# Two-layer hybrid backbone on one core: raw slots of their own for the second half of the output weights, gate rows written to DRAM in the first branch, six first tiles in the last layer

## The chip, the cores and the metric

The kernel runs on one core of a Trainium2 chip. The metric is the device time of one launch in microseconds (us). Before the change the median of 3 runs is 2333.93 us (2331.47 to 2334.76).

## The reference, cut to what matters

Two layers work on 1024 latent tokens and 256 context tokens of width 1024, all in float32. Each layer normalizes and modulates its input, projects it into an attention, a convolution and a recurrent branch, and merges the three branches. The change touches only the merge and what follows it:

```python
y = stack([yb * silu(gb) for yb, gb in zip(ys, gs)])
proj = einsum('btnw,nwd->btnd', y, w_branch)          # three products 512 -> 1024
g = sigmoid(h @ w_gate + b_gate)                      # three gates per channel
out = sum(proj * g, over the branches) @ w_out        # the output product, 1024 -> 1024
x = layer_norm(ALPHA * x + gate * out) * ln_g + ln_b  # gate: one row per stream
```

The first layer does this for context and latent tokens, the last layer for latent tokens alone, since only they are returned. `gate` is a row of 1024 numbers; latent and context tokens have one each.

## The kernel before, in words

Every float32 product is made of three matmuls: each operand is split into a high part and a remainder (`hi`, `lo`), and hi*hi, hi*lo and lo*hi are added up in PSUM. A weight tile (class `Wt`, `load` at L330) costs one 512 KB DMA on SP's queue into a slot called `raw`, one ACT copy that makes `whi`, and one DVE subtraction that makes `wlo`. The pool `W` has NWL = 2 slots for `raw` and NW = 4 each for `whi` and `wlo`.

A layer has two phases. Phase 1 does the projections and the branches and leaves the branch outputs (`y_d`) and the gates (`th_d`) in DRAM. Phase 2 (L1140) does the merge in two stages:

- Branch stage (`gemm`, loop over `i, b in enumerate(BR)`): for each of three branches four weight units (`dp`), each with two output chunks (`dd`), each with the token groups: NT_C (256 context tokens, first layer only), NT_0 and NT_1 (512 latent tokens each). A group is 12 matmuls. DVE multiplies the PSUM result with the gate tile `thl`, which SP loads into three slots in turn, and adds it to `m`. In the third branch (`i == 2`) ACT and DVE split the finished chunk of `m` into the tiles that are the left operand of the output product.
- Output stage: the tokens are cut into tiles of 128 (ten in the first layer, eight in the last). A half (`half_of(q, ch)`) is the product of tile q with one half of the output columns, 24 matmuls in four steps `kp` of 6, each with one weight tile. `w0` (four tiles) is the first half of `w_out` and `w1` (four tiles) the second. Then DVE multiplies by the gate tile `gt`, adds the residual `xp` and takes statistics; after the second half `norm` normalizes the tile and writes it out.

The program text makes the weight tiles of the output stage in this order: `w0[0]` and `w0[1]`, fetched ahead in the branch stage; then, after the pool `a` of the branch stage is closed and the pool `c` opened in its place, `w1[0..3]`; then `w0[2]` and `w0[3]`. `w1` keeps `whi` and `wlo` in pool `c`, but its `raw` slots are the two of `W`. The halves are worked through in an order set by `first = 4`: the first halves of four tiles, their second halves, then both halves of each later tile.

Pool `a` holds, by address, three `yst` slots (6 KB per partition), three `thl` slots (6 KB) and the branch operands `yy`. Pool `c` reuses that room; a tile in it waits only for the tiles that it covers.

The gate row comes from `gate_rows` (L1130), called in the third branch: a PE transpose of a column tile, a DVE copy into `grow`, a DMA of `grow` to `gate_d` in DRAM, and two DMAs that read it back, spread over all partitions, into `gt`. In the first layer it is called after `dp` 1 (context) and `dp` 3 (latent), in the last after `dp` 0.

The order on each engine is fixed before the run. A planner (class `Driver`) picks by estimated times which stream emits its next step; a scheduler then goes by program order among the instructions whose operands and slots are ready in its own simulated time. A load can so be put ahead of earlier program text if its slot is free. On the chip each engine and each DMA-issuing queue then runs its list in order.

Of the kernel before, what the change touches and what calls it, by code (L numbers as in the profile page):

```python
# [8 lines left out]
F32 = mybir.dt.float32  # L9
# [26 lines left out]
NS, NHF, NW, NWL, NMX, NYST = 10, 14, 4, 2, 8, 3  # L36
# [153 lines left out]
def kernel(  # L190
# [12 lines left out]
    W = ctx.enter_context(tc.tile_pool(name="wts", bufs=1))  # L203
# [15 lines left out]
    def f32(ap):  # L219
        return ap.bitcast(F32)  # L220

    def psum(n=512, name="ps"):
        return PM.tile([128, n], F32, tag="mm", name=name, bufs=4)
# [97 lines left out]
    class Wt:  # L321
# [6 lines left out]
            self.ap, self.ready = drv_.side(lambda: self.load(src, a, b, home or W))  # L328

        def load(self, src, a, b, home):  # L330
            raw = W.tile([128, a, b], F32, tag="raw", name="raw", bufs=NWL)
            sp.dma_start(out=raw, in_=src)
            hi = home.tile([128, a, b], F32R, tag="whi", name="whi", bufs=NW)
            lo = home.tile([128, a, b], F32R, tag="wlo", name="wlo", bufs=NW)
            act.activation(out=hi, in_=raw, func=AF.Copy)
            dve.tensor_tensor(out=lo, in0=raw, in1=f32(hi), op=ALU.subtract)
            return hi, lo
# [789 lines left out]
        drv_.run([lru(), att_values(), att_scores(), lru_in(), lru_out(), att_proj(), att_out(), conv(), gates()], PRIO[l])  # L1127
        assert wlive[0] == 0 and sl.used == 0 and hl_.used == 0 and pl_.used == 0

    def gate_rows(l, s, dst):  # L1130

        row = SM.tile([128, 128], F32, tag="grow", name="grow")
        ps = psum()
        pe.transpose(ps[0:KD, 0:128], ada[l][:, 16:24, s], ident)
        dve.tensor_copy(row[0:KD], ps[0:KD, 0:128])
        sp.dma_start(out=gate_d[l][s].rearrange("(k p) -> k p", p=128), in_=row[0:KD])
        for i in range(2):
            sp.dma_start(out=dst[i], in_=gate_d[l][s][i * 512:i * 512 + 512].partition_broadcast(128))

    def phase2(l, open_a, open_b, open_c):  # L1140

        last = l == DEPTH - 1
        groups = [NT_0, NT_1] if last else [NT_C, NT_0, NT_1]
# [73 lines left out]
        gts, lnw = {}, []  # L1217

        def gemm():
            tfetch()  # L1220
            wfetch(2)
            ms, mg = {}, {}
            for i, b in enumerate(BR):
                for dp in range(4):
                    if i == 0:
                        for nt in groups:
                            if nt is NT_C:
                                ms[dp, 0] = mc("m").rearrange("p (d n) -> p d n", d=2)
                                continue
                            yield ("pe", xq.room())  # L1230
                            xq.take()
                            ms[dp, nt[0]] = mx("m", [128, 2, 512])
                    w = wnext()
                    wfetch(2)
                    for dd in range(2):
                        dch = dp * 2 + dd
                        for nt in groups:
                            ti, t0, n = nt
                            while (i, ti) not in yt_ or any(e[:2] == (i, nt) for e in yq):
                                yield ("act", drv_.t["pe"] + LAG_Y)  # L1240
                                ysplit()
                            if i == 2 and (ti not in mg):
                                mg[ti] = alloc_h(ti, n)
                            tfetch()
                            th = tq.pop(0)
                            yield ("pe", w.ready)
                            y = yt_[i, ti]
                            ps = psum()
                            c_ = 0
                            for k in range(4):  # L1250
                                for a, v in ((0, 0), (0, 1), (1, 0)):
                                    pe.matmul(out=ps[:, 0:n], lhsT=w[a][:, k, dd * 128:dd * 128 + 128], rhs=y[:, v, k, :],
                                              start=(c_ == 0), stop=(c_ == 11))
                                    c_ += 1
                                if k == 1:
                                    yield "pe"
                            mm = ms[dp, ti][:, dd, 0:n]
                            dst = mm if i == 0 else th[:, 0:n]
                            dve.scalar_tensor_tensor(out=dst, in0=th[:, 0:n], scalar=1.0, in1=ps[:, 0:n], op0=ALU.add,
                                                     op1=ALU.mult)  # L1260
                            if i:
                                dve.tensor_tensor(out=mm, in0=mm, in1=dst, op=ALU.add)
                            if i == 2:
                                split(mm, mg[ti][0][:, dch, :], mg[ti][1][:, dch, :])
                        if dp:
                            for _ in range((len(groups) + 1) // 2 if dd else len(groups) - (len(groups) + 1) // 2 + 1):
                                if yq and yq[0][0] == i + 1:
                                    yield "act"
                                    ysplit()
                    w.free()  # L1270
                    if i == 2:
                        xq.give(2)
                        if dp in ((0,) if last else (1, 3)):
                            s_ = 1 if dp == 1 else 0
                            gts[s_] = mc("gt"), mc("gt")
                            gate_rows(l, s_, gts[s_])
                        if dp == 3:
                            xq.take(2)
                            lnw.extend((mx("lng", [128, D]), mx("lnb", [128, D])))
                            sp.dma_start(out=lnw[0], in_=ln_g[l].partition_broadcast(128))  # L1280
                            sp.dma_start(out=lnw[1], in_=ln_b[l].partition_broadcast(128))
                        elif dp:
                            for _ in range(2):
                                xq.take()
                                xfetch()
            sa.close()
            sc, RC = open_c()
            pools.append((sc, RC))
            w1 = [Wt(w_out[l][kp * 256:kp * 256 + 256, 512:1024].rearrange("(k p) n -> p k n", p=128), 2, 512, RC)
                  for kp in range(4)]  # L1290
            w0 = [wnext() for _ in range(4)]
            sts = {}
            first = 4

            def half_of(q, ch):
                nt, t = tiles[q]
                ti, n = nt[0], nt[2]
                if ch == 0:
                    while len(xps) <= q:
                        yield ("pe", xq.room())  # L1300
                        xq.take()
                        xfetch()
                cq = slice(ch * 512, ch * 512 + 512)
                ws = (w0, w1)[ch]
                ps = None
                for kp in range(4):
                    yield ("pe", ws[kp].ready)
                    if ps is None:
                        ps = psum()
                    for k in range(2):  # L1310
                        for a, v in ((0, 0), (0, 1), (1, 0)):
                            pe.matmul(out=ps, lhsT=mg[ti][a][:, 2 * kp + k, t * 128:t * 128 + 128], rhs=ws[kp][v][:, k, :],
                                      start=(kp == 0 and k == 0 and a == 0 and v == 0), stop=(kp == 3 and k == 1 and a == 1))
                tt = RC.tile([128, 512], F32, tag="tt", name="tt", bufs=2)
                dve.tensor_tensor(out=tt, in0=ps, in1=gts[1 if ti == 0 else 0][ch], op=ALU.mult)
                dve.scalar_tensor_tensor(out=xps[q][:, cq], in0=xps[q][:, cq], scalar=ALPHA, in1=tt, op0=ALU.mult, op1=ALU.add)
                if ch == 0:
                    sts[q] = SM.tile([128, 2, 6], F32, tag="st1", name="st1", bufs=8)
                    ln_half(xps[q], sts[q], 0)
                else:  # L1320
                    fin.append((nt, t, xps[q], sts[q]))
                    if t == n // 128 - 1:
                        done.add(ti)

            order = [(q, ch) for ch in range(2) for q in range(first)]
            order += [(q, ch) for q in range(first, len(tiles)) for ch in range(2)]
            for q, ch in order:
                yield from half_of(q, ch)
            for w in w0 + w1:
                w.free()  # L1330
# [129 lines left out]
```

## Time and profile before

| | |
|---|---|
| median of 3 runs | 2333.93 us |
| profiled execution | 2332.71 us, span 2330.9 us, mean granted TensorE clock 0.986 |
| PE | 2257.4 us busy, 97% of the span, 11344 matmuls |
| DVE | 1679.5 us, 72% |
| ACT | 1003.3 us, 43% |
| POOL | 87.0 us, 4% |
| SP's DMA queue (q1) | 226.06 MB; ACT's (q10) 51.92 MB |

Phase 2 of the first layer runs from about 1022 to 1317 us, that of the last layer from about 2080 us to the end. PE is busy nearly throughout, so a change can gain only where PE stands still or runs at the lower of its two clock levels, or in the last 9 us, where it has finished.

### The profile page before, as it was taken

How to read it: one execution, taken by the hardware profiler on the slowest of the kernel's cores; microseconds unless marked ns; L12 is line 12 of the kernel's file. 1: busy time of each engine (PE TensorE's matmuls, PEld its weight loads, DVE VectorE, ACT ScalarE, POOL GpSimd, SP SyncE). 2: the span in 40 equal slices, each digit the busy share in tenths (PEclk: the TensorE clock that was granted, in tenths of full speed). 3: DMA queues.
4: the chain of work that ended last, by engine and by line, in shares of the span. 5: the costliest groups of instructions: out<-in, count | busy, mean ns of one | idle time of the engine just before them, and what ended most of it. 6: DMA issues, size and time to landing. Idle time of an engine off the chain costs nothing.

```text
span 2330.9 us, 29959 instructions
## 1 busy us (share of the span) xinstructions
PE 2257.4 (97%) x11344; PEld 1875.9 (80%) x11344; DVE 1679.5 (72%) x2453; ACT 1003.3 (43%) x1642; POOL 87.0 (4%) x140
## 2 busy tenths in 40 slices
PE   7999999999999999999989999999999999999988
PEld 2888888888888887888868788888888878778876
DVE  5579967868859874445658749869787887656666
ACT  3555563244444575321122644555344456542110
POOL 1000000000000111000001100000000011000001
PEclk8999999999999999999999999999999999999999
DMA  7222323433334232655551222224433334346531
GB/s 271 77 73 100 118 72 121 140 111 113 100 120 132 84 102 88 213 175 167 152 171 73 92 67 66 84 91 131 140 90 103 102 106 136 99 145 212 173 118 76
DMA packets 270945, 279.90 MB, mean 120 GB/s; under 512 B 19768, under 2 KB 199888, under 8 KB 270800
## 3 DMA queue, kind: packets, MB, share of 16 engines
q1 hardware_dynamic: 242288, 226.06, 31.1%
q10 hardware_dynamic: 28512, 51.92, 6.4%
q8 instruction: 89, 1.46, 0.3%
q14 instruction: 56, 0.46, 0.1%
HBM read 203.04 MB, written 74.88 MB: 119 GB/s over the span
## 4 chain that ended last, share of the span: by engine, by line
PE 84%; DVE 6%; DMA 5%; ACT 3%; issue 2%; SPq 1%; POOLq 0%; POOL 0%; ACTq 0%; DVEq 0%
PE ps L73 78%; PE yp L73 3%; PE pt L73 2%; DMA yst<-yd 1%; DVE acc L73 1%; DMA raw<-in_w_out_dram 1%; DMA raw<-in_w_ada_dram 1%; DVE P L73 1%; DMA thl<-th 1%; PE pa L73 1%; DMA qd<-qd 1%; DVE wlo L73 1%; ACT whi L73 1%; DVE pl L73 1%; PE p L73 0%
## 5 line engine op out<-in xcount | busy, mean ns | idle before, releaser
L73 PE MATMUL ps<-hlhi,whi 128*128 128x512 f32 x1728 | 682.2, 396 | 2.2 <-DVE gs L73 1.0
L73 PE MATMUL ps<-hllo,whi 128*128 128x512 f32 x1728 | 679.1, 393 | 0.0
L73 PE MATMUL ps<-hlhi,wlo 128*128 128x512 f32 x1728 | 677.5, 393 | 0.0
L73 PEld LDWEIGHTS ps<-hlhi,wlo 128*128 128x128 f32 x1728 | 326.3, 189 | 67.9 <-issue 0.4
L73 PEld LDWEIGHTS ps<-hlhi,whi 128*128 128x128 f32 x1728 | 326.9, 189 | 66.7 <-DVE pl L73 2.1
L73 PEld LDWEIGHTS ps<-hllo,whi 128*128 128x128 f32 x1728 | 326.6, 189 | 62.9 <-issue 0.7
L73 DVE SCALAR_TENSOR_TENSOR acc<-u,cwt,acc 128x1296 f32<-128x1296 f32 (+1 forms) x240 | 342.9, 1429 | 2.2
L73 ACT ACTIVATE whi<-raw 128x1024 fp32r<-128x1024 f32 x180 | 190.0, 1057 | 348.0 <-PE ps L73 295.9
L73 DVE TENSOR_TENSOR wlo<-raw,whi 128x1024 fp32r<-128x1024 f32 x180 | 220.7, 1227 | 111.4 <-ACT whi L73 109.4
L73 PE MATMUL ps<-yy,whi 128*128 128x512 f32 (+1 forms) x960 | 271.5, 368 | 2.9 <-DVE m L73 2.9
L73 PEld LDWEIGHTS ps<-yy,whi 128*128 128x128 f32 x960 | 173.6, 188 | 33.8 <-DVE m L73 3.6
L73 PE MATMUL ps<-yy,wlo 128*128 128x512 f32 (+1 forms) x480 | 176.5, 368 | 0.0
L73 ACT ACTIVATE ph<-pt 128x512 fp32r<-128x512 f32 x160 | 93.9, 591 | 132.2 <-PE pt L73 126.8
L73 DVE TENSOR_TENSOR pl<-pt,ph 128x512 fp32r<-128x512 f32 x160 | 109.2, 686 | 52.7 <-ACT ph L73 51.2
L73 PE MATMUL ps<-hchi,whi 128*128 128x256 f32 x480 | 135.6, 283 | 1.3 <-ACT whi L73 0.6
L73 ACT ACTIVATE P<-P,nm 128x640 f32<-128x640 f32 (+1 forms) x128 | 101.9, 797 | 80.4 <-DVE nm L73 80.4
L73 PE MATMUL ps<-hchi,wlo 128*128 128x256 f32 x480 | 135.2, 282 | 1.0 <-DVE wlo L73 1.0
L73 PE MATMUL ps<-hclo,whi 128*128 128x256 f32 x480 | 134.5, 280 | 0.0
L73 DVE CUSTOM_DVE_ANT_0 P<-ps,m_mid,nsink 128x640 f32<-128x640 f32 (+1 forms) x112 | 93.1, 860 | 42.2 <-PE ps L73 40.7
L73 PE MATMUL ps<-whi,hlhi 128*128 128x512 f32 x256 | 100.6, 397 | 6.3 <-ACT whi L73 6.3
L73 ACT ACTIVATE tg<-ps,drv 128x512 f32<-128x512 f32 (+1 forms) x120 | 76.4, 637 | 67.9 <-PE ps L73 67.3
L73 PEld LDWEIGHTS ps<-yy,wlo 128*128 128x128 f32 x480 | 90.4, 188 | 15.2
(205 smaller groups left out, 3402.7 us busy)
## 6 DMA issues: line engine op xcount, KB each, us to landing
raw<-in_w_in_dram SPq DMA_DIRECT2D x60, 512.0 KB
raw<-in_w_ada_dram SPq DMA_DIRECT2D x48, 512.0 KB
raw<-in_w_gate_dram SPq DMA_DIRECT2D x48, 512.0 KB
th<-tg ACTq DMA_DIRECT2D x96, 256.0 KB
thl<-th SPq DMA_DIRECT2D x96, 256.0 KB
yd<-gs ACTq DMA_DIRECT2D x48, 256.0 KB
yst<-yd SPq DMA_DIRECT2D x48, 256.0 KB
raw<-in_w_branch_dram SPq DMA_DIRECT2D x24, 512.0 KB
```

The source lines that it names most:

```text
L73: return f(*a, **k)
```

## The change

Three edits. The `raw` tiles of weights with a home of their own go to that home, with NW = 4 slots; only `w1` has such a home (pool `c`), which so grows from 36 to 52 KB per partition. `gate_rows` is cut in two: `gate_out` (transpose, copy, write to DRAM) runs in the first branch, ahead of `dp` 1 for latent tokens and in the first layer ahead of `dp` 2 for context; `gate_in` (the two reads) stays where `gate_rows` was called. In the last layer `first` is 6 instead of 4.

```diff
         def load(self, src, a, b, home):
-            raw = W.tile([128, a, b], F32, tag="raw", name="raw", bufs=NWL)
+            raw = home.tile([128, a, b], F32, tag="raw", name="raw", bufs=NWL if self.own else NW)
             sp.dma_start(out=raw, in_=src)
...
-    def gate_rows(l, s, dst):
+    def gate_out(l, s):
 
         row = SM.tile([128, 128], F32, tag="grow", name="grow")
         ps = psum()
         pe.transpose(ps[0:KD, 0:128], ada[l][:, 16:24, s], ident)
         dve.tensor_copy(row[0:KD], ps[0:KD, 0:128])
         sp.dma_start(out=gate_d[l][s].rearrange("(k p) -> k p", p=128), in_=row[0:KD])
+
+    def gate_in(l, s, dst):
         for i in range(2):
             sp.dma_start(out=dst[i], in_=gate_d[l][s][i * 512:i * 512 + 512].partition_broadcast(128))
...
                 for dp in range(4):
+                    if i == 0 and 0 < dp < len(groups):
+                        gate_out(l, dp - 1)
...
-                            gate_rows(l, s_, gts[s_])
+                            gate_in(l, s_, gts[s_])
...
-            first = 4
+            first = 6 if last else 4
```

## Rows read from the trace of the kernel before

**Rows 1.** Busy time by stretch: length, PE, PEld, DVE, ACT, POOL, clock, DMA, GB/s.
```profile
1217.00:1317.00 100.00, 100.00 (x464) 83.11 (x463) 82.26 (x147) 28.22 (x51) 16.39 (x17) 1.00 0.24 83
1317.00:1327.00 10.00, 5.13 (x42) 4.70 (x41) 9.00 (x16) 9.47 (x22) 1.10 (x2) 0.92 0.41 127
1327.00:1333.00 6.00, 6.00 (x20) 4.99 (x19) 2.23 (x7) 5.43 (x12) 0.67 (x4) 0.56 0.12 50
1333.00:1700.00 367.00, 365.80 (x1723) 305.88 (x1722) 279.33 (x287) 186.65 (x255) 2.99 (x19) 1.00 0.29 92
1700.00:2070.00 370.00, 359.35 (x1758) 298.14 (x1757) 286.67 (x462) 188.56 (x349) 16.89 (x14) 0.99 0.34 106
```
**Rows 2.** The same view, at the two starts of the output stage.
```profile
1201.40:1211.80 10.40, 0.01 (x1) 0.02 (x1) 2.49 (x3) 3.17 (x3) 0.00 (x0) 0.72 0.52 178
1211.80:1216.50 4.70, 4.70 (x12) 3.69 (x13) 2.41 (x2) 1.06 (x1) 0.00 (x0) 0.53 0.45 130
...
2237.60:2243.90 6.30, 0.01 (x1) 0.01 (x1) 2.48 (x3) 2.33 (x3) 0.00 (x0) 0.71 0.46 160
2243.90:2247.10 3.20, 3.20 (x8) 2.52 (x9) 2.24 (x2) 1.06 (x1) 0.00 (x0) 0.50 0.03 12
```
**Rows 3.** Chain of waits, first layer: start, us, what the chain ran through.
```profile
1192.90 2.97 DMA gd<-grow
...
1196.83 7.79 DMA raw<-in_w_out_dram
...
1204.64 1.06 ACT whi L73
...
1205.72 1.24 DVE wlo L73
...
1206.98 3.68 DMA raw<-in_w_out_dram
...
1211.79 86.94 PE ps L73 x384
```
**Rows 4.** Chain of waits, last layer.
```profile
2231.55 5.18 DMA raw<-in_w_out_dram
...
2239.10 3.66 DMA raw<-in_w_out_dram
...
2243.89 77.95 PE ps L73 x336
```
**Rows 5.** SP's queue in order of time, first layer (start, us of issuing).
```profile
1165.63 0.38 SPq L332 DMA_DIRECT2D raw<-in_w_out_dram  x1
...
1184.16 3.03 SPq L1200 DMA_DIRECT2D thl<-th  x2
...
1196.83 11.81 SPq L332 DMA_DIRECT2D raw<-in_w_out_dram  x4
```
**Rows 6.** SP's queue in order of time, last layer.
```profile
2210.22 0.38 SPq L332 DMA_DIRECT2D raw<-in_w_out_dram  x1
...
2221.80 0.32 SPq L1200 DMA_DIRECT2D thl<-th  x1
```
**Rows 7.** PE in order of time: first matmul of the output stage, first layer.
```profile
1190.16 0.48 PE L73 MATMUL ps<-whi,hchi 128*128 128x512 f32 x1
```
**Rows 8.** The same in the last layer.
```profile
2226.56 0.39 PE L73 MATMUL ps<-whi,hlhi 128*128 128x512 f32 x1
```
**Rows 9.** All instructions on `grow`: duration minimum/median/maximum in ns, first and last start.
```profile
L73 DVE COPY grow<-ps x3: 272/272/274, 1164.2 to 2195.2; 8x128 f32<-8x128 f32 x3
```
**Rows 10.** ACT in order of time, last layer: loads of the last two residual tiles.
```profile
2270.27 5.74 ACTq L1214 DMA_DIRECT2D xp<-xs_d  x2
```
**Rows 11.** DVE in order of time, last layer: gate multiplications of the halves.
```profile
2267.46 0.69 DVE L73 TENSOR_TENSOR tt<-ps,gt 128x512 f32<-128x512 f32 x1
...
2272.90 0.69 DVE L73 TENSOR_TENSOR tt<-ps,gt 128x512 f32<-128x512 f32 x1
...
2321.86 0.69 DVE L73 TENSOR_TENSOR tt<-ps,gt 128x512 f32<-128x512 f32 x1 [3.29 <-PE ps L73]
```

## The prediction

> **What bounds the kernel now.** I read the page first: PE is busy for 97% of the span, so only its idle time, its time at the lower clock and the 9 us after its last matmul can be won. The list of who waited for whom, kept to PE, then shows one entry far above all others inside the kernel: `ps` waiting for ACT's `whi`, 10.4 us once and 6.3 us once. Both lie at the start of an output stage. The windows there show PE doing nothing from 1201.4 to 1211.8 and from 2237.6 to 2243.9, and right behind each gap a stretch with a granted clock of 0.53 and 0.50, the 1.2 GHz level, for 4.7 and 3.2 us [rows 2].
>
> The chain of waits says what PE waits for. In the first layer: a load of `w_out` of 7.79 us, its `whi`, its `wlo` of 1.24 us, then the next load, of 3.68 us, which could only be issued when that `wlo` had freed a `raw` slot; then PE goes on [rows 3]. In the last layer it is the same with 5.18 and 3.66 us [rows 4]. SP's queue and the program text tell which weights these are. Eight loads of `w_out` are made per layer. The first two are `w0[0]` and `w0[1]`. The next two, issued 16 to 25 us and more ahead of the output stage (the second of each pair at 1165.63 and 2210.22), are `w1[0]` and `w1[1]`, since `w1` stands before the rest of `w0` in the text and shares `W`'s two slots [rows 5, 6]. Their `whi` belongs to pool `c`, which opens only when the branch stage is done, so they hold both slots for all that time. `w1[2]`, `w1[3]`, `w0[2]`, `w0[3]` follow from 1196.83 on. PE needs `w0[2]` at once and `w1` only after four halves: the load needed first comes seventh.
>
> **Edit 1, raw slots for w1.** `w1` leaves the two slots of `W`, so the early loads (the one at 1165.63 and its predecessor; 2210.22 and its predecessor) are now `w0[2]` and `w0[3]` [rows 5, 6]. `W`'s four `whi` slots come free as the weight units of the third branch end; the last of them ends where the output stage starts, 1190.16 and 2226.56 [rows 7, 8]. So `w0[3]` is ready 1.06 + 1.24 = 2.3 us later (durations of [rows 3]), 1192.5 and 2228.9. The first half asks for it after 18 of its 24 matmuls. A half takes 5.44 us (distance of two gate multiplications [rows 11]), so that is 4.1 us in: 1194.2 and 2230.6. It is in time by 1.7 us in both layers, and both gaps go.
>
> What goes with them: 10.4 + 6.3 = 16.7 us of idle PE, and the slow stretches behind them, 4.7 x (1 - 0.53) = 2.2 us and 3.2 x (1 - 0.50) = 1.6 us [rows 2]. Sum 20.5 us.
>
> What is late next is `w1`, four loads that now start when pool `c` opens. In the first layer SP is through with `thl` at about 1187.2 [rows 5], `raw` covers slots of `yst` and `thl` and a part of `yy` that are free by then or within some 5 us, and the two reads of the gate row go ahead, so the loads start at about 1188. The price of a load in such a row is between 3.68 and 7.79 us [rows 3]. Four of them end at 1202.7 or at 1219.2, plus 2.3 us for the split: 1205.0 or 1221.5. The last of them is needed 4 x 5.44 + 4.1 = 25.9 us into the stage, at 1216.0. I take the low end plus a little, in time, because 7.79 is the first of four loads, issued while two residual tiles and the gate reads were under way; high end: 5.5 us late and 2.2 us of slow clock, 7.7 us. In the last layer, starting at 2222.1 behind the last `thl` [rows 6], even the high end is 2255.6 against 2263.3 (with six first halves, 6 x 5.44 + 4.1 behind 2226.56): nothing.
>
> The Trainium skill, page "DMA: Bandwidth & Descriptors", section "Issuing engines are not separate DMA queues", speaks against this edit: copies run on the same 16 DMA engines and interleave whoever issues them, so more slots bring no more bandwidth. The trace bears it out with 7.79 against 3.68 us for the same 512 KB [rows 3]; by that rule the four loads of `w1` gain nothing from four slots, and it is the high end above and the first rival below.
>
> In the first layer the loads for the next phase also find `W`'s slots free earlier and go ahead of `w1`: one or two more loads among the last `thl` loads, 3.7 to 7.8 us each. PE was full there, with DVE behind it having slack; I take nothing, bound 3 us.
>
> **Edit 2, gate rows.** Three transposes and three copies of 0.27 us [rows 9] and three writes move from the third branch to the first; the number of instructions is the same. They lie beside matmuls in both places, on DVE and SP, with PE giving a few tenths of a us to the transposes in either place. What goes is SP's stand behind the write: 2.97 us before the reads and behind them the load of 1196.83 [rows 3]. That is on the chain now, but the slot for that load came free at almost the same time (`wlo` of `w1[0]`), so alone the edit is worth under 1 us, and with edit 1 it only starts `w1` earlier, already used above. Bounds -1 to +1 us, taken as 0. The reads now find the row long written.
>
> **Edit 3, six first tiles.** The matmuls are the same. It lets `w1` come 2 x 5.44 = 10.9 us later, which the sum above doesn't need in the last layer unless loads take the high price (with four the need would be at 2252.5, 3.1 us before 2255.6). Against it: six second halves in a row, each with a full normalization on DVE. DVE now keeps the pace of 5.44 us in such a row without falling behind [rows 11], and four PSUM buffers stand between. The residual tiles 6 and 7 are loaded when tiles 0 and 1 are out; now at 2270.27 [rows 10], then, with the gap of 8 us gone and two halves more in front, at about 2273, needed at 2226.56 + 13 x 5.44 = 2297. Nothing, bound 1 us. The tail from the last gate multiplication, 2321.86 [rows 11], to the end at 2330.9 stays 9 us.
>
> **Behind the first layer's output stage** everything should shift by 10.4 + 2.2 = 12.6 us. From 1217 to 1317 PE is full and DVE 82% [rows 1], so DVE isn't the bound that takes the gain. At the change to layer 1 PE idles for 4.9 us and then runs at 0.56 for 6 us [rows 1], 7.5 us in all, waiting for the normalized last tiles; I let that stand, though DVE gets its first work earlier in the stage and may shorten it.
>
> **Sum.** 2332.71 (the profiled execution's own time, span 2330.9 and 1.8 around it) - 20.5 = 2312.2. The median of the runs shown is 1.2 above that execution, so on its scale 2313.4; I say 2313.
>
> **Rivals.** First, `w1` is late in the first layer, by the high price: 2313 + 7.7 = 2321. For it: the transfers of that stretch already share the DMA engines; DVE's list is fixed, and a `wlo` that waits holds back the evacuation of PSUM. Against: 11 us of room at the low price. Second, the change doesn't do what it says: `w0[2]` still stands behind `w1` on SP, as in the text. Then it follows four loads: 1188 + 5 x 3.68 + 2.3 = 1208.7 and 2222.1 + 18.4 + 2.3 = 2242.8, against 1211.8 and 2243.9: 4.2 us gained, 2329.7. Against: loads in `W` run far ahead of the text now [rows 5]. Third, slower: the order of the whole program is planned anew, and layer 1's first phase, 737 us long, comes out worse. It idles 1.2 + 10.65 = 11.9 us now; its worse part 2.9% [rows 1]. If all of it idled at twice that share, 42.7 us, the time would be 2313 + 30.8 = 2344. It decides for slower from 25 us more idle. For it: those 370 us hang on many short waits; against: nothing in the change touches that phase but its start.
>
> **How the numbers follow.** What a measurement here can tell from no change is about 0.2%, 4.7 us: faster is under 2329.3, slower above 2338.6. Chances: forecast 0.68, with its own range 2308 to 2318; first rival 0.14; second 0.06; third 0.07; and 0.05 for a better end than forecast, the 7.5 us at the change of layers gone as well, 2305.5. The range that holds 8 in 10 takes the forecast, the first rival and part of the better end: 2306 to 2325. Faster is the forecast, the first rival and the better end, 0.87; same the second rival, 0.06; slower the third, 0.07.
>
> **What would show it.** In the changed profile: no wait of `ps` for `whi` over 1 us at the two output stages, clock 1.00 through both; the fourth load of `w_out` issued before the stage starts and four more from its start; no stand of SP between gate write and gate reads; the first DVE gate multiplication about 6 us into the stage. A wait of PE in the fifth half means the first rival; one in the first half the second; idle PE spread over layer 1's first phase the third. The forecast is wrong if both gaps go and the time falls by less than 12 us.

## The result and the profile after

The changed kernel takes 2307.78 us (median of 4 runs, 2307.39 to 2308.43), the kernel before in the same session 2332.7 us (2327.21 to 2334.76): ratio 0.9897, 95% interval 0.9879 to 0.9915. A second session gave 0.9905 (0.9889 to 0.9921), 2311.03 against 2333.0 us. The forecast was 2313 us, with 2306 to 2325 as its range and 2308 to 2318 for its main case: the first median lies just below that main case, the second in it.

The list of who waited for whom, kept to PE, has lost its first entry. In the kernel before it begins so (in total, times, longest):

```profile
PE ps L73 <- ACT whi L73: 17.3, 4, 10.4
PE yp L73 <- ACT ph L73: 8.6, 9, 2.2
PE ps L73 <- DVE crow L73: 5.8, 1, 5.8
PE ps L73 <- ACT hf L73: 4.9, 2, 3.9
```

In the changed kernel the second entry stands first, and no wait for `whi` is left over 0.3 us:

```profile
PE yp L73 <- ACT ph L73: 9.1, 9, 2.3
PE ps L73 <- DVE crow L73: 5.8, 1, 5.8
PE ps L73 <- ACT hf L73: 4.8, 2, 3.9
```

The windows of the changed kernel, in the order start of the first output stage, its bulk, layer change (two), phase 1 of layer 1 in two parts, last output stage (two) and the tail (length, PE, PEld, DVE, ACT, POOL, clock, DMA, GB/s):

```profile
1189.50:1203.00 13.50, 13.50 (x61) 11.10 (x60) 5.90 (x8) 4.20 (x5) 0.00 (x0) 1.00 0.82 278
1203.00:1303.00 100.00, 100.00 (x464) 83.16 (x463) 85.36 (x149) 30.48 (x54) 16.39 (x17) 1.00 0.23 81
1303.00:1313.15 10.15, 5.35 (x44) 4.92 (x43) 8.95 (x16) 9.48 (x22) 1.09 (x2) 0.86 0.41 126
1313.15:1319.15 6.00, 6.00 (x23) 5.01 (x22) 2.22 (x7) 5.43 (x12) 1.13 (x5) 0.67 0.18 61
1319.15:1700.00 380.85, 379.65 (x1793) 317.82 (x1792) 289.15 (x307) 193.88 (x270) 2.57 (x18) 1.00 0.29 93
1700.00:2055.00 355.00, 344.20 (x1692) 285.16 (x1691) 278.30 (x445) 182.06 (x336) 17.04 (x15) 0.99 0.34 106
...
2209.90:2231.00 21.10, 21.10 (x94) 17.46 (x94) 14.11 (x18) 5.39 (x6) 0.00 (x0) 1.00 0.29 105
2231.00:2297.00 66.00, 65.92 (x291) 54.25 (x289) 44.47 (x65) 0.00 (x0) 10.38 (x7) 1.00 0.19 72
2297.00:2306.00 9.00, 0.00 (x0) 0.00 (x0) 4.87 (x7) 0.00 (x0) 1.46 (x1) 0.68 0.14 58
```

Where PE stood still and then ran at half speed [rows 2], it is now busy all the time at clock 1.00. Phase 1 of layer 1 idles 1.2 and 10.8 us, as before [rows 1].

SP's queue of the changed kernel shows the new order ahead of the first output stage (start, us of issuing):

```profile
1150.34 0.38 SPq L332 DMA_DIRECT2D raw<-in_w_out_dram  x1
...
1164.09 0.38 SPq L332 DMA_DIRECT2D raw<-in_w_out_dram  x1
...
1188.57 0.32 SPq L1140 DMA_DIRECT2D gt<-gd  x1
1193.01 0.38 SPq L332 DMA_DIRECT2D raw<-in_w_in_dram  x1
1193.44 2.29 SPq L332 DMA_DIRECT2D raw<-in_w_out_dram  x4
```

The loads of 1150.34 and 1164.09 are `w0[2]` and `w0[3]`; the four of 1193.44 are `w1`, one behind the other with no wait between. SP no longer stands between gate write and gate reads [rows 3]. It stands in another place, from 1188.9 to 1193.0: the load of the next phase (`w_in`), which comes ahead of `w1`, needs the shared slot that `w0[3]` holds until its `wlo` is done at 1193.0 (first line below). DVE of the changed kernel, in order of time, shows when the weights are ready:

```profile
1191.76 1.22 DVE L73 TENSOR_TENSOR wlo<-raw,whi 128x1024 fp32r<-128x1024 f32 x1
...
1200.34 1.23 DVE L73 TENSOR_TENSOR wlo<-raw,whi 128x1024 fp32r<-128x1024 f32 x1 [5.37 <-ACT whi L73]
1201.48 0.69 DVE L73 TENSOR_TENSOR tt<-ps,gt 128x512 f32<-128x512 f32 x1
...
1207.25 1.20 DVE L73 TENSOR_TENSOR wlo<-raw,whi 128x1024 fp32r<-128x1024 f32 x1
```

The stage starts at 1189.37. `w0[3]` is split at 1193.0, `w1` between 1201.6 and 1208.5, that is 12.2 to 19.1 us into the stage.

There are as many matmuls in every kernel here, so the start of a matmul can be set against that of the matmul with the same number in the first trace of the kernel before. The table gives the differences in us, worked out from the traces (minus: earlier); the column heads are times in the kernel before, just ahead of and behind each output stage (1190 and 1300, 2226 and 2300) and at places between:

```
                    60    1020    1040    1190    1300    1500    2060    2090    2226    2300
changed          -1.37   -1.19   -0.88   -0.99  -13.80  -14.44  -14.65  -16.27  -16.84  -24.90
changed, 2nd     -1.59   -1.37   -1.47   -1.59  -14.38  -14.86  -14.96  -16.58  -17.00  -25.06
before, 2nd      -1.03   -0.53   -0.07   -0.07   -0.04   -0.28   -0.53   -2.12   -2.27   -1.41
raw_slots_only   -1.43   -1.34    0.90    0.90  -11.99  -11.78  -11.69  -11.72  -12.36  -20.42
w0_before_w1     -0.76    2.65    2.61    2.61  -10.27  -10.34  -10.60  -10.63  -10.07  -18.13
order_gate_six   -0.73    0.12    2.29    2.17  -10.32  -10.33  -10.26  -10.28   -9.62  -17.68
without_six      -0.34   -0.14    0.32    0.21  -12.60  -13.19  -14.08  -14.07  -15.03  -23.09
two_first_tiles  -0.45    0.19    0.89    0.77  -10.14   -9.94   -9.86  -11.45  -12.04  -20.10
gate_rows_only   -1.22   -2.04    1.60    1.48   -4.00   -4.22   -4.38   -6.01   -2.89   -1.88
one_gate_read    -0.18    0.92    1.29    1.29   -2.39   -2.60   -2.65   -4.27   -3.74   -3.61
six_first_only   -0.05    1.12    3.65    3.65    4.30    4.39    4.41    2.79    3.13    3.80
```

In the changed kernel the first output stage gives 13.80 - 0.99 = 12.8 us, the last 24.90 - 16.84 = 8.1 us, 20.9 us together; the other 4.0 us lie elsewhere.

### The profile page after: what moved, and what is told of

It reads as the page before. It is cut to its first block, busy times and chain, and to the rows that moved or that the text cites. A ratio compares the mean times of both kernels' runs of the same rounds, so it can differ in the third digit from the quotient of the medians.

```text
span 2306.0 us, 29961 instructions
## 1 busy us (share of the span) xinstructions
PE 2249.3 (98%) x11344; PEld 1871.8 (81%) x11344; DVE 1678.9 (73%) x2453; ACT 1003.4 (44%) x1642; POOL 86.7 (4%) x140
## 4 chain that ended last, share of the span: by engine, by line
PE 88%; DVE 5%; ACT 2%; DMA 2%; issue 2%; SPq 0%; POOLq 0%; POOL 0%; ACTq 0%; DVEq 0%
PE ps L73 82%; PE yp L73 3%; PE pt L73 2%; PE pa L73 1%; DVE acc L73 1%; DMA raw<-in_w_ada_dram 1%; DVE P L73 1%; DVE pl L73 1%; DVE wlo L73 1%; DMA yst<-yd 1%; ACT whi L73 0%; DMA qd<-qd 0%; DVE xp L73 0%; PE p L73 0%; ACT hf L73 0%
## 5 line engine op out<-in xcount | busy, mean ns | idle before, releaser
L73 PE MATMUL pt<-ident,P 128*128 128x128 f32 x640 | 97.2, 274 | 3.1 <-DVE pl L73 1.4
```

Source lines behind the costliest of these rows:

```text
L73: return f(*a, **k)
```

## Experiments

The theory: PE stood because `w0[2]` was loaded behind `w1`; edit 1 cures that and gives all, edits 2 and 3 nothing. The rivals: the number of slots counts, or the gate row, or the six tiles.

**Edit 1 alone** (`raw_slots_only`):

```diff
-            raw = W.tile([128, a, b], F32, tag="raw", name="raw", bufs=NWL)
+            raw = home.tile([128, a, b], F32, tag="raw", name="raw", bufs=NWL if self.own else NW)
```

> Edit 1 alone: w1 gets four raw slots in pool c; gate rows and first = 4 as before. Theory (w1 holds both shared raw slots until pool c opens, so w0[2] comes seventh): both gaps of 10.4 and 6.3 us and the slow clock behind them go, and nearly the whole fall of the changed kernel comes from this line: 2307 to 2311 us, ratio 0.989 to 0.991. Rival (the gate write that SP stands behind is a good part of it): 2318 to 2326 us, since the stand of 3 us and a late w1 remain.

2311.48 against 2335.09 us, ratio 0.9905 (0.9889 to 0.9921). The time is 0.5 us over the expected range, the ratio inside it. In its trace the kernel gains 12.9 and 8.1 us in the two output stages, all that the three edits gain there.

**The order alone** (`w0_before_w1`): in the text of the kernel before, `w0` is completed ahead of `w1`, and the two slots stay shared.

```diff
+            w0 = [wnext() for _ in range(4)]
...
-            w0 = [wnext() for _ in range(4)]
```

> The kernel before with two statements exchanged: all of w0 is made before w1; raw slots stay two, gate rows and first as before. Theory (it is the order of the loads, not the number of slots): w0[2] and w0[3] get the early loads, both gaps go; w1 comes two by two after pool c opens, the last ready about 20 us into the stage, needed after 25.9 us: 2308 to 2312 us, ratio 0.989 to 0.991. Rival (the slots count): w1 is late and the wait moves to the fifth half, 5 to 10 us per layer: 2315 to 2328 us.

2314.57 us, ratio 0.9908 (0.9893 to 0.9923): 12.9 and 8.1 us in the stages, with no slot added. The time is 2.6 us over the expected range; the ratio is inside it. The order is the cause; own slots are one way to change it.

**Edit 2 alone** (`gate_rows_only`):

```diff
-    def gate_rows(l, s, dst):
+    def gate_out(l, s):
...
+    def gate_in(l, s, dst):
...
+                    if i == 0 and 0 < dp < len(groups):
+                        gate_out(l, dp - 1)
...
-                            gate_rows(l, s_, gts[s_])
+                            gate_in(l, s_, gts[s_])
```

> Edit 2 alone: gate rows written in the first branch, raw slots and first = 4 as before. Theory: the load of 1196.83 also waits for a slot that wlo of w1[0] frees 0.4 us before SP is free, so the gap shrinks by under 1 us: ratio 0.999 to 1.001. Rival: SP's stand sets the gap, 3 us in the first layer and about 1 us in the last less: 2328 us, ratio 0.998.

2328.25 against 2335.09 us, ratio 0.9978 (0.9968 to 0.9989): 2.6 to 7.5 us, more than the forecast's bound of 1 us. The time is the one that the rival named, but the trace does not show the rival's reason. The chain of waits of this kernel in the first layer (start, us, what it ran through):

```profile
1195.10 1.24 DVE wlo L73
...
1196.36 4.87 DMA raw<-in_w_out_dram
...
1201.25 1.07 ACT whi L73
...
1202.34 1.24 DVE wlo L73
...
1203.60 3.72 DMA raw<-in_w_out_dram
```

The wait behind the gate write cost what the forecast said: the load starts at 1196.36 in place of 1196.83, since its slot comes free with the `wlo` of 1195.10. But it takes 4.87 us and not 7.79 [rows 3]. SP's queue shows the difference: the last gate read is issued at 1188.85 here; in the kernel before two reads of 256 KB are issued at 1195.93, right ahead of the load. The first output stage gains 5.5 us in this trace, 1.5 of them because PE comes to it later (table); the last stage gains nothing, where the rival expected about 1 us.

**One read in place of two** (`one_gate_read`, from the kernel before; both halves of the output columns use the gates of the first half):

```diff
-        for i in range(2):
-            sp.dma_start(out=dst[i], in_=gate_d[l][s][i * 512:i * 512 + 512].partition_broadcast(128))
+        sp.dma_start(out=dst[0], in_=gate_d[l][s][0:512].partition_broadcast(128))
...
-                            gts[s_] = mc("gt"), mc("gt")
+                            gts[s_] = (mc("gt"),) * 2
```

> The kernel before, with one read of the gate row per stream in place of two: both halves of the output columns use the first 512 gates, so the result is another. The stand of SP behind the gate write stays. It asks why edit 2 alone gained 3 to 5 us in the first layer. There the load behind the gate reads began 0.5 us earlier than before (1196.36 against 1196.83) but took 4.87 us in place of 7.79. Theory A (the two reads of 256 KB, issued just ahead of the load, slow it): with one read the load takes about 6.3 us, PE's longest wait falls from 10.4 to about 8.5 us, and the first layer's output stage gains 1.5 us; total 2 us. Theory B (the stand behind the write is what counts): load 7.8 us, wait 10.4 us, no gain beyond the 0.4 us of one issue less. Both expect nothing in the last layer, where the reads lie far ahead of the stage.

2331.56 against 2333.0 us, ratio 0.9991 (0.9980 to 1.0001). SP's queue and, below it, the chain of waits of this kernel:

```profile
1193.12 0.28 SPq L1136 DMA_DIRECT2D gd<-grow  x1
1196.12 0.33 SPq L1137 DMA_DIRECT2D gt<-gd  x1
1196.59 10.09 SPq L332 DMA_DIRECT2D raw<-in_w_out_dram  x4
```

```profile
1196.59 6.07 DMA raw<-in_w_out_dram
...
1205.03 3.67 DMA raw<-in_w_out_dram
```

The stand of 3.0 us behind the write is still there, and the load takes 6.07 us, beside 7.79 with two reads and 4.87 with none in front. The other two traces with both reads right in front, `before_again` and `six_first_only`, have the long load too:

```profile
1197.45 7.82 DMA raw<-in_w_out_dram
...
1201.02 8.24 DMA raw<-in_w_out_dram
```

Theory A holds: what edit 2 removes in this place is above all the transfer ahead of the load. PE's longest wait is 7.2 us, lower than the 8.5 expected, because PE came to the stage 1.3 us later than in the first trace while this chain did not; for the same reason the stage gains 3.7 us in the trace and not 1.5. The time of the whole kernel can't be told from no change.

**Edit 3 alone** (`six_first_only`):

```diff
-            first = 4
+            first = 6 if last else 4
```

> Edit 3 alone: six first tiles in the last layer, the rest as before. Theory: what PE waits for in the last layer is w0[2], which the order of the later halves doesn't touch; gap of 6.3 us stays, ratio 0.999 to 1.001. Rival: only four PSUM buffers and four tiles at work make the wait as long as it is; with six tiles more PE work could stand before the wait, up to 2 x 2.7 us less.

2335.93 us, ratio 1.0003 (0.9992 to 1.0014): no change that these runs can tell, as forecast.

**Less edit 3** (`without_six`, beside the changed kernel once more, `all_three_again`): edits 1 and 2, `first = 4`.

> The changed kernel once more, so that the two variants of it beside it are compared on one chip. Both theories: the ratio to the kernel before is again 0.990 (0.988 to 0.992). What tells something is where the gain lies: the order theory says that the first layer's output stage gives 12.9 us and the last layer's 8.1 us between the same matmuls of the two kernels, 21.0 in all, and that the other 3 to 4 us of the first profile were differences between executions, so here anything between -2 and +4 us there. The rival, that the change also gains elsewhere, expects 3 to 4 us there once more.

> Edits 1 and 2 with the four first tiles in both layers, so the changed kernel less edit 3. Theory: w1's last split ends 13.2 us into the last layer's output stage in the changed kernel, and with four first tiles it is needed 4 x 5.44 + 4.1 = 25.9 us into it, so six tiles buy nothing: within 1 us of the changed kernel, no wait of PE for a weight split over 1 us in either output stage. Rival: six first tiles cover a late w1, and without them PE waits some 3 us in the fifth half of the last layer and loses 1 to 1.5 us of slow clock: 4 us slower than the changed kernel.

`all_three_again` has the ratio 0.9905 (0.9889 to 0.9921), `without_six` 0.9906 (0.9890 to 0.9922). Both gain the same 12.8 and 8.1 us in the stages, and in neither does PE wait over 1 us for a weight split. Edit 3 buys nothing on top either. Outside the stages `all_three_again` gains 4.2 us, over the +4 of the first expectation and as its rival said; `before_again` below asks about that.

**The second half pulled forward** (`two_first_tiles`): the changed kernel with `first = 2` in both layers.

```diff
-            first = 6 if last else 4
+            first = 2
```

> The changed kernel with two first tiles in both layers, so that w1 is needed 2 x 5.44 = 10.9 us into the output stage (its last quarter 15.0 us). Theory (w1 is the next thing that is late, and only in the first layer): there w1's quarters are split between 12.2 and 19.1 us into the stage, so PE waits 1.3 us for the first and, the wait shared along the four, about 4 us in all, with 1 to 2 us of slow clock behind it: 5 to 6 us slower than the changed kernel. In the last layer the quarters are split by 13.2 us and needed from 10.9 to 15.0: no wait. Rival (loads with four slots are always far ahead, the order of the halves is free): within 1 us of the changed kernel.

2312.64 us, ratio 0.9914 (0.9900 to 0.9928): in time it can't be told from the changed kernel, so the trace must decide. The first stage gains 10.9 us in place of 12.8, the last is unchanged. The window of this kernel in which `w1` is late:

```profile
1199.90:1208.00 8.10, 6.81 (x29) 4.97 (x28) 4.12 (x5) 3.99 (x4) 0.00 (x0) 1.00 0.78 293
```

`w1` is the next late thing, and in the first layer alone, as the theory said. But PE stands for 1.3 us in this window and the stage loses 1.9 in all, not 5 to 6: the clock stays at 1.00 in this window. That PE loses so little of a `w1` that is up to 4 us late is probably because it works at two halves in turn (below); no run takes that apart.

**Another edit 1** (`order_gate_six`): edits 2 and 3, and the order of `w0_before_w1` in place of own slots.

> The changed kernel with another edit 1: w1 keeps the two shared raw slots, and w0[2], w0[3] are made ahead of it in the text. Theory (order is the cause, own slots are one way to get it): 12.9 us over the first layer's output stage and 8.1 us over the last layer's, as with own slots, no wait of PE for a weight split over 1 us; w1's loads then go two at a time through the shared slots, which its distance of 25.9 us covers; ratio 0.990 to 0.991. Rival (four slots also matter): w1 is late in the first layer, PE waits 2 to 5 us in the fifth half, stage gain 8 to 10 us.

2313.48 against 2332.91 us, ratio 0.9912 (0.9896 to 0.9929); 12.5 and 8.1 us in the stages. The last quarter of `w1` is split 20 us into the first stage, with two slots in place of four. Four slots are not needed; 0.3 us less in the first stage is no more than two traces of one kernel can differ by (next run).

**The kernel before, profiled again** (`before_again`):

> The kernel before, unchanged, profiled once more. It asks whether the 3 to 4 us that the changed kernel has gained in both its profiles outside the two output stages (1.4 and 1.6 us in the first 60 us, the rest at the start of the last layer's merge) belong to the change. Theory (differences between executions): the start of the same matmul against the first profile of the kernel before differs by up to 2 us in either direction at those two places, and by under 0.3 us over each output stage. Rival (the change gained them): within 0.3 us at all of them.

2331.3 us, one run. Its start again comes out 1.0 us earlier and the stretch from 2060 to 2090 1.6 us earlier than in the first trace, with nothing changed; the changed kernel has 1.4 and 1.6 there. So 2.6 of the 4.0 us outside the stages are also seen without the change. By the table the five other kernels without the gaps lie between 2.9 us lost and 2.2 gained outside the stages, so the 4.0 are no fixed gain of the change; what makes up the rest of them is open. That each stage repeats within 0.3 us held for the first (0.03) but not for the last (0.86 us slower).

## Why the prediction was right

**Cause and edit 1.** Right. Both gaps were the order of the eight loads; edit 1 alone and the bare order each give the whole. Forecast were 12.6 and 7.9 us, 20.5 in all; measured 12.8 and 8.1. The time is 5 us under the point, 4.0 of them gained outside the stages, where two traces of the same kernel already differ by 2.6. That part is chance as far as the runs show: the better end that the forecast had at 2305.5 needed the change of layers to get shorter, and it hardly did (below). In the second session the median fell by 22 us, near the 20.5 that were forecast.

**`w0[3]` in time.** Forecast 2.3 us behind the start of the stage; measured 1193.0 - 1189.37 = 3.6, and PE did not wait. The forecast asked for it at 4.1 us, since it assumed that PE finishes one half before it starts the next. PE doesn't: the first gate multiplication was forecast 6 us into the stage and came at 12.1 us in the first layer and 9.0 in the last, the next one 2.3 us behind it:

```profile
2218.75 0.69 DVE L73 TENSOR_TENSOR tt<-ps,gt 128x512 f32<-128x512 f32 x1 [1.35 <-PE ps L73]
...
2221.09 0.68 DVE L73 TENSOR_TENSOR tt<-ps,gt 128x512 f32<-128x512 f32 x1
```

The first half is done 9.0 us into the stage where one costs 5.44, and the second at most 2.3 us later: they were worked on in turn. That step was wrong, in the direction that gives more room. In the first layer there is more to it: DVE waits 5.37 us for the first `whi` of `w1` with a multiplication queued behind. PE had other PSUM buffers to write and didn't stand.

**`w1` in time.** Forecast between 1205.0 and 1221.5, needed at 1216.0, with a start at 1188. The loads started later, at 1193.4. The forecast had seen that a load for the next phase could go ahead of `w1`, but it priced that as a transfer, taken at nothing with a bound of 3 us; what it cost was SP's stand of 4.1 us for the slot of `w0[3]`. From first issue to last split it then took 15.0 us, under the 4 x 3.68 + 2.3 = 17.0 of the low price. The last split ended at 1208.5, 19.1 us into the stage: 4.3 us behind the low end of the forecast and 6.8 ahead of the need of 25.9. The high price did not come: 7.79 was not the price of a load among many but of one behind the gate reads, as the forecast had suspected when it took the low end. That four slots are no faster than two agrees with the runs as far as they go: `order_gate_six` with two slots has `w1` only 1 us later in the stage.

Beside the high price the forecast named the page "DMA: Bandwidth & Descriptors" of the Trainium skill, section "Issuing engines are not separate DMA queues", by which DMAs of all issuers run on the same 16 DMA engines and interleave. The traces agree in that the load took 7.79, 6.07 and 4.87 us with two, one and no reads right in front; the late `w1` that the forecast drew from it did not come.

**Edit 2.** Together with edit 1 it is worth nothing in time, as forecast, and splits `w1` some 3 us earlier in the stage (22.0 us in with edit 1 alone, 19.1 with all). Alone it was mis-sized: the forecast said under 1 us, measured 2.6 to 7.5. The step that failed there is that the slot came free at almost the same time and the edit alone was "worth under 1 us": it priced when the load starts (0.5 us earlier) and not how long it then takes with the two reads out of its way (2.9 us less).

**Edit 3, tail and layer change.** The tail is 9.0 us as forecast. The layer change idles 10.15 - 5.35 = 4.8 us and loses 6.0 x (1 - 0.67) = 2.0 at the lower clock, 6.8 against the 7.5 that the forecast left as they were.

**Rivals.** `w1` late: not at four or six first tiles; brought on with two, at 1.9 us and not 7.7. Not doing what it says: excluded by SP's queue. A worse phase 1: from 1500 to 2060 the differences of the changed kernel move by only 0.2 us (table).

## What to carry to other kernels

Where a stage starts with a wait, list the loads in the order in which the queue issues them and set beside it the order in which they are needed: a load parked in a shared slot ahead of its time costs the one that could have gone in front. Exchanging two statements was worth 21 us here, as much as four more buffers. And price a moved DMA twice, once for when it lets its successor start and once for how much longer the successor takes beside it.

## What was not expected of the hardware

Two reads of 256 KB, issued right ahead of a 512 KB load, made it 2.9 us longer (7.79 against 4.87), one made it 1.2 us longer (6.07). The reads spread a row over all partitions, but nothing here shows that the spreading is what costs: the two together are as many bytes as one such load, which took 3.68 us with little else under way [rows 3].

The two traces of the kernel before differ by 0.9 to 1.6 us in three places (the start, 2060 to 2090, the last output stage) and by up to 0.5 between the others, so a difference of that size between two traces isn't the change's until a second trace shows it.

Larger ones need care too. Four kernels lose 2.2 to 3.6 us between 1020 and 1040, where the first merge starts; one is `six_first_only`, whose edit acts some 1200 us later. Their traces differ from the other eight by the granted clock there. The first line is of the kernel before, the others of `raw_slots_only`, `order_gate_six`, `six_first_only` and `gate_rows_only`:

```profile
1028.00:1040.00 12.00, 9.86 (x55) 8.45 (x54) 7.02 (x13) 3.04 (x5) 0.00 (x0) 1.00 0.72 226
...
1028.00:1040.00 12.00, 9.24 (x42) 7.58 (x41) 5.65 (x11) 2.38 (x4) 0.00 (x0) 0.86 0.65 202
...
1028.00:1040.00 12.00, 9.33 (x40) 7.55 (x39) 6.63 (x11) 2.49 (x4) 0.00 (x0) 0.86 0.66 215
...
1028.00:1040.00 12.00, 8.97 (x39) 7.28 (x38) 6.23 (x11) 3.11 (x5) 0.00 (x0) 0.86 0.69 217
...
1028.00:1040.00 12.00, 8.92 (x31) 7.01 (x31) 4.71 (x8) 1.69 (x3) 0.00 (x0) 0.72 0.58 184
```

PE waits once there for DVE's `m`, 2.7 to 3.1 us in these four and 2.0 to 2.8 in the others, and only in the four does the clock fall behind it. Why it falls in one trace and not in another after waits of nearly the same length stays open. `gate_rows_only` loses 3.1 us in the same way in the last layer's merge: a wait of 1.9 us, then 0.86 between 2095 and 2107. What `w0_before_w1` loses before 1020, 3.4 us, is not explained.
